# Two transformer blocks on one core: attention values computed transposed, exponentials normalised and gated before their transposes

## The chip, the cores and the metric

The kernel runs on one core of a Trainium2 chip. The metric is the device time of one execution in microseconds (us). Before the change the median of three runs is 2130.94 us (2128.68 to 2131.86).

## The reference, cut to what matters

The program computes two transformer blocks on 512 tokens of width 1024. The first (sliding-window attention, a gated recurrence, retrieval of experts) is not touched. The second projects its normalised input to queries, keys and values of two attentions. In the first one (eight heads of width 64, two groups of keys and values) three softmax branches are added, each with a sigmoid gate per token and head; the compressed branch has 31 keys, and its rows without a valid key give zeros. With 512 tokens and 16 selected blocks of 64 the selected and the window branch are both plain causal attention over all keys.

```python
o_cmp = jnp.einsum('bghsn,bngd->bsghd', p_cmp.astype(vc.dtype), vc)
...
g = jax.nn.sigmoid(gate_logits.astype(jnp.float32)).reshape(B, S, G, HPG, N_BRANCH).astype(q.dtype)
o = g[..., 0:1] * o_cmp + g[..., 1:2] * o_slc + g[..., 2:3] * o_win
...
s = (jnp.einsum('bqhd,bkhd->bhqk', qn, k_nope) + jnp.einsum('bqhd,bkd->bhqk', qr, k_rot)).astype(jnp.float32) * scale
p = masked_softmax(s, key_idx[None, :] <= tc[:, None])
return jnp.einsum('bhqk,bkhd->bqhd', p.astype(v.dtype), v)
...
mixed = jnp.concatenate([o_nsa * jax.nn.silu(z_nsa), o_mla * jax.nn.silu(z_mla)], axis=-1)
x = x + gate[:, None, :] * (mixed @ w_out[l])
return rms_norm_2(x, final_norm_g)
```

The second attention (called MLA) has eight heads with queries and keys of width 96 and values of width 64.

## The kernel before

The second block's attention runs in the trace from about 1793 to 2092 us. Its input `h` lies transposed in two parts, high and low, and every product of `h` with a weight is three matmuls (L105, L106, L107: high·high, low·high, high·low). These are the "fill" records below; they have 512 columns.

Attention is cut into units. A `Unit` is a pair of heads for one tile of 128 queries, `tt`; its keys are the first n = (tt+1)·128. It has three steps. *Scores* (L1371, mask L1373) go into two PSUM banks; VectorE takes the maxima (L1376), ScalarE the exponentials with their sums (L1379, tile `sm_p`). *Turn* transposes the exponentials on TensorE in pieces of 128 keys (L1387) and copies them to SBUF (`sm_pt`; copies alternate between ScalarE, L63, and VectorE, L65). *Values* multiplies the transposed exponentials, as the stationary operand, by the values (L1394), 64 columns for each head and key block, so that the queries come out on the partitions. A `Blocks` unit does the same for the compressed branch with all eight heads at once (L1409, L1413, turn L1429, values L1437 with values laid out block-diagonally by L1689). Sums are inverted after the last unit of a branch (`nsa_done`: reciprocal L1454, gate L1457), and the finished outputs are weighed with them (L1355) and added up by GpSimd (L1463); MLA likewise (L1495, L1497). `mix` transposes the outputs on TensorE (L1548), multiplies them by silu(z) (L1551) and splits them into high and low parts for the output projection.

The order on TensorE is written by hand; the other engines' orders are made by a scheduler from the same program. `attention()` (L1520) takes the units in the order of a table (key tiles 0 and 1, compressed tiles 0 and 1, key 2, compressed 2, MLA 0 and 1, key 3, compressed 3, MLA 2 and 3; a key tile has eight units, an MLA tile four). At each step it issues the turn of the unit before, the scores of the present one, some fill, and the values of the unit two back. The fill is a generator: projections for MLA and the gates, the compressed keys (`blocks`; `fold` L1642 adds position vectors to a projection, L1663 is the hidden layer, its two results on the two column halves), columns of z0, MLA heads (transposes L1709), columns of z1 with a silu at the end (L1803, on ScalarE), the mix of the tiles and the output projection of tiles 0 and 1. `weave_us` draws from it by a number of microseconds that the table gives each unit. The output projection can start only when tiles 0 and 1 of both attentions are mixed. The output projection of tiles 2 and 3 and the last normalisation follow at the end.

Of the kernel before, what the change touches and what calls it, by code (L numbers as in the profile page):

```python
# [17 lines left out]
OP = mybir.AluOpType  # L18
# [1239 lines left out]
def block2(K, x, h, wq, out):  # L1258
    nc, tc, A = K.nc, K.tc, K.A
    with ExitStack() as ctx:  # L1260
# [10 lines left out]
        oN = P.tile([128, NT, 512], F32, name="oN")  # L1271
# [4 lines left out]
        vc = P.tile([128, 2, 4, 64], F32, name="vc")  # L1276
        nc.gpsimd.memset(vc, 0.0)
# [71 lines left out]
        def pair_cols(hh):  # L1349
            j, g = hh % 4, hh // 4  # L1350
            return slice(j * 128 + g * 64, j * 128 + (g + 1) * 64)

        def weigh(dst, o, f):

            nc.vector.tensor_tensor(dst.rearrange("p (j g d) -> p g j d", g=2, d=64),  # L1355
                                    o.rearrange("p (j g d) -> p g j d", g=2, d=64),
                                    f.rearrange("p (g j) -> p g j", g=2)[:, :, :, None].to_broadcast([128, 2, 4, 64]),
                                    op=OP.mult)

        class Unit:  # L1360

            post = needs = None

            def __init__(self, tt, q, k, sums, v, o):
                self.tt, self.q, self.k, self.sums, self.v, self.o = tt, q, k, sums, v, o

            def scores(self):
# [9 lines left out]
                self.p = [T.tile([128, 512], F32, name="sm_p", bufs=2) for _ in range(2)]  # L1377
                for i in range(2):
                    nc.scalar.activation(self.p[i][:, :n], sc[i][:, :n], AF.Exp, bias=m[i], accum_out=self.sums[i])  # L1379
# [11 lines left out]
            def values(self):  # L1391
                for i in range(2):
                    for kb in range(self.tt + 1):
                        nc.tensor.matmul(self.o(i), self.pt[i][:, kb * 128:(kb + 1) * 128], self.v(i, kb), start=kb == 0,  # L1394
                                         stop=kb == self.tt)

        class Blocks:
# [3 lines left out]
            def __init__(self, tt, csum, o):  # L1401
                self.tt, self.csum, self.o = tt, csum, o

            def scores(self):
# [11 lines left out]
                pc = self.pc = T.tile([128, 512], F32, name="sm_p", bufs=2)[:, :256].rearrange("p (j n) -> p j n", n=32)  # L1416
                nc.gpsimd.memset(pc[:, :, NCMP:], 0.0)
                for g in range(2):
                    hs = slice(4 * g, 4 * g + 4)
                    nc.vector.tensor_reduce(cx[:, hs], p3[g], axis=AX.X, op=OP.max)  # L1420
                    nc.vector.tensor_tensor(pc[:, hs, :NCMP], p3[g], cx[:, hs, None].to_broadcast([128, 4, NCMP]),
                                            op=OP.subtract)
                nc.scalar.activation(pc[:, :, :NCMP], pc[:, :, :NCMP], AF.Exp)
                nc.vector.tensor_reduce(self.csum, pc[:, :, :NCMP], axis=AX.X, op=OP.add)

            def turn(self):
                tp = K.bank("tp")
                for g in range(2):
                    nc.tensor.transpose(tp[:, g * 128:(g + 1) * 128],  # L1429
                                        self.pc[:, 4 * g:4 * g + 4].rearrange("p j n -> p (j n)"), K.ident)  # L1430
                self.pt = T.tile([128, 512], F32, name="sm_pt", bufs=2 * LAG + 2)
                K.copy(self.pt[:, :256], tp[:, :256])

            def values(self):
                o = self.o().rearrange("p (j g d) -> p g j d", g=2, d=64)
                for g in range(2):
                    nc.tensor.matmul(o[:, g], self.pt[:, g * 128:(g + 1) * 128], vc[:, g], start=True, stop=True)  # L1437
# [520 lines left out]
```

## Time and profile before

| what | us |
|---|---|
| median of 3 runs | 2130.94 |
| the profiled execution | 2125.71 |
| its span | 2123.9 |
| TensorE busy | 2007.9 |
| VectorE busy | 1558.1 |
| ScalarE busy | 883.4 |

The profiled execution is 5.2 us shorter than the median of the runs, and its span covers all but 1.8 us of it. Engine names in the rows: PE is TensorE's matmul side, PEld its weight loads, DVE VectorE, ACT ScalarE, POOL GpSimd. In a timeline row the number in brackets is the idle time before, with what ended it. Ends of matmuls are modelled, so distances between starts are the better measure.

### The profile page before, as it was taken

To read this page: it belongs to the slowest core of one execution; us is meant where nothing else is said; L and a number is where in the kernel's file an instruction comes from. 1 tells how busy PE (TensorE), PEld (TensorE's weight loads), DVE (VectorE), ACT (ScalarE), POOL (GpSimd) and SP (SyncE) were. 2 spreads that over 40 slices of the span, in tenths; PEclk is the share of its full clock that TensorE was granted. 3 is DMA by queue.
4 is the path that set the end of the run, shared out by engine and by line. 5 is a ranking of instruction groups with operands and counts; after the bars stand their busy time and mean duration, and the time that the engine had idled before them with its cause. 6 is when DMAs were issued, how large, how long until landed. Compare 5 with 4: busy or idle time off the path is not lost.

```text
span 2123.9 us, 29904 instructions
## 1 busy us (share of the span) xinstructions
PE 2007.9 (95%) x11220; PEld 1723.1 (81%) x11220; DVE 1558.1 (73%) x2998; ACT 883.4 (42%) x1368; POOL 489.7 (23%) x408
## 2 busy tenths in 40 slices
PE   8999898999977889999999999999999999989998
PEld 6878676788866878899999999999988877777776
DVE  4457765569999997777777787887878776545557
ACT  4454423333333776333333333333334453444544
POOL 0000001220452000444444444444432101011000
PEclk9999999999988999999999999999999999999999
DMA  4224333442321556998999989999988772211012
GB/s 153 78 79 139 112 117 109 159 139 80 90 80 60 213 214 238 338 328 310 327 329 308 338 304 330 325 315 323 315 292 287 269 236 70 76 40 51 31 51 79
DMA packets 154376, 410.49 MB, mean 193 GB/s; under 512 B 13789, under 2 KB 63733, under 8 KB 150774
## 3 DMA queue, kind: packets, MB, share of 16 engines
q1 hardware_dynamic: 113332, 247.07, 34.4%
q0 software_dynamic: 37440, 136.33, 18.5%
q10 hardware_dynamic: 3458, 25.17, 3.1%
q8 instruction: 88, 1.44, 0.3%
q14 instruction: 58, 0.48, 0.1%
HBM read 378.64 MB, written 29.37 MB: 192 GB/s over the span
## 4 chain that ended last, share of the span: by engine, by line
PE 81%; DVE 12%; ACT 3%; DMA 2%; issue 2%; POOL 1%; ACTq 0%; DVEq 0%; POOLq 0%
PE ps_mm L105 13%; PE ps_mm L106 13%; PE ps_mm L107 13%; PE ps_o L105 7%; PE ps_o L107 6%; PE ps_o L106 6%; PE ps_tp L107 3%; PE ps_tp L106 3%; PE ps_tp L105 3%; PE ps_mm L1000 2%; PE ps_o L1394 2%; PE ps_sc L1371 2%; PE ps_tp L1387 1%; DVE wlo L69 1%; DVE sum L891 1%
## 5 line engine op out<-in xcount | busy, mean ns | idle before, releaser
L68 ACT ACTIVATE whi<-raw 128x1024 fp32r<-128x1024 f32 (+1 forms) x363 | 382.5, 1056 | 658.6 <-issue 429.5
L69 DVE TENSOR_TENSOR wlo<-raw,whi 128x1024 fp32r<-128x1024 f32 (+1 forms) x339 | 415.9, 1229 | 192.5 <-ACT whi L68 191.3
L105 PE MATMUL ps_o<-hT_hi,whi 128*128 128x384 f32 x992 | 342.6, 345 | 13.1 <-ACT act L725 13.1
L107 PE MATMUL ps_o<-hT_hi,wlo 128*128 128x384 f32 x992 | 336.9, 340 | 0.1
L106 PE MATMUL ps_o<-hT_lo,whi 128*128 128x384 f32 x992 | 336.1, 339 | 0.0
L1032 POOL DMA_INDIRECT gath<-in_peer_u_dram,idx x128 | 179.5, 1402 | 376.0 <-DVE junk L1040 181.6
L1032 POOL DMA_INDIRECT gath<-in_peer_v_dram,idx x128 | 176.2, 1376 | 257.0 <-DVE acc L1047 213.6
L105 PE MATMUL ps_mm<-hT_hi,whi 128*128 128x512 f32 (+1 forms) x544 | 222.5, 409 | 0.0
L107 PE MATMUL ps_mm<-hT_hi,wlo 128*128 128x512 f32 (+1 forms) x544 | 216.3, 398 | 0.0
L106 PE MATMUL ps_mm<-hT_lo,whi 128*128 128x512 f32 (+1 forms) x544 | 215.7, 397 | 0.0
L105 PEld LDWEIGHTS ps_o<-hT_hi,whi 128*128 128x128 f32 x992 | 189.8, 191 | 17.2 <-ACT act L725 13.9
L105 PE MATMUL ps_mm<-whi,wh 128*128 128x512 f32 x512 | 200.0, 391 | 2.1 <-ACT wh L68 2.1
L106 PE MATMUL ps_mm<-wlo,wh 128*128 128x512 f32 x512 | 201.6, 394 | 0.4 <-DVE wlo L69 0.4
L107 PE MATMUL ps_mm<-whi,wl 128*128 128x512 f32 x512 | 201.7, 394 | 0.0
L106 PEld LDWEIGHTS ps_o<-hT_lo,whi 128*128 128x128 f32 x992 | 189.6, 191 | 3.3
L107 PEld LDWEIGHTS ps_o<-hT_hi,wlo 128*128 128x128 f32 x992 | 189.1, 191 | 1.0 <-POOL wlo L69 0.6
L1047 DVE SCALAR_TENSOR_TENSOR acc<-gath,w,acc 128x1024 f32<-128x1024 f32 x127 | 162.8, 1282 | 5.6 <-DMA gath<-in_peer_v_dram,idx 3.5
L1040 DVE SCALAR_TENSOR_TENSOR junk<-gath,h 128x1024 bf16<-128x1024 f32 x128 | 156.6, 1223 | 6.8 <-DMA gath<-in_peer_u_dram,idx 4.2
L107 PEld LDWEIGHTS ps_mm<-hT_hi,wlo 128*128 128x128 f32 (+1 forms) x544 | 103.7, 191 | 23.6
L105 PEld LDWEIGHTS ps_mm<-hT_hi,whi 128*128 128x128 f32 (+1 forms) x544 | 103.8, 191 | 21.5 <-ACT dec L508 0.4
L1002 ACT ACTIVATE gst<-ps_mm 128x512 f32<-128x512 f32 x96 | 104.1, 1127 | 40.0 <-PE ps_mm L1000 39.6
L106 PEld LDWEIGHTS ps_mm<-hT_lo,whi 128*128 128x128 f32 (+1 forms) x544 | 103.8, 191 | 20.6 <-DVE hT_lo L69 0.2
(483 smaller groups left out, 3542.5 us busy)
## 6 DMA issues: line engine op xcount, KB each, us to landing
raw<-in_peer_uT_dram SPq DMA_DIRECT2D x128, 512.0 KB
raw<-in_peer_v_dram SPq DMA_DIRECT2D x128, 512.0 KB
raw<-in_w_in_dram SPq DMA_DIRECT2D x59, 512.0 KB
gates_dram<-gst ACTq DMA_DIRECT2D x24, 1024.0 KB
x<-gates_dram SPq DMA_DIRECT2D x32, 768.0 KB
raw<-in_ada_w_dram SPq DMA_DIRECT2D x24, 512.0 KB
raw<-in_w_out_dram SPq DMA_DIRECT2D x24, 512.0 KB
raw<-in_w_peer_q_dram SPq DMA_DIRECT2D x16, 512.0 KB
```

Source lines behind the costliest of these rows:

```text
L68: self.nc.scalar.activation(hi, src, AF.Copy)
L69: (engine or self.nc.vector).tensor_tensor(lo, src, hi.bitcast(F32), op=OP.subtract)
L105: mm(out, a[0], b[0], start=start, stop=False)
L106: mm(out, a[0], b[1], start=False, stop=False)
L107: mm(out, a[1], b[0], start=False, stop=stop)
L1000: nc.tensor.matmul(ps_, hot[:, 1, t // 2, :, t % 2], Ag[:, i, t // 2, :, t % 2], start=i == 0, stop=i == 2)
L1002: nc.scalar.activation(st[:, :, t0:t0 + 4].rearrange("p a t -> p t a"), p.rearrange("p (t a) -> p t a", t=4), AF.Copy)
L1032: nc.gpsimd.indirect_dma_start(out=gath[i], out_offset=None, in_=A["peer_u" if i < NG // 2 else "peer_v"], in_offset=bass.IndirectOffsetOn ...
L1040: nc.vector.scalar_tensor_tensor(junk, g, 1.0, h0, op0=OP.mult, op1=OP.mult, accum_out=act0[:, k:k + 1])
L1047: nc.vector.scalar_tensor_tensor(acc0, g, w0[:, k:k + 1], acc0, op0=OP.mult, op1=OP.add)
L1371: nc.tensor.matmul(sc[i][:, :n], self.q[i], self.k[i], start=True, stop=False)
L1394: nc.tensor.matmul(self.o(i), self.pt[i][:, kb * 128:(kb + 1) * 128], self.v(i, kb), start=kb == 0, stop=kb == self.tt)
```

## The change

Values change operands: the values are the stationary operand (128 keys by 64), the transposed exponentials move (128 columns), and the two heads of a pair write the two halves (`i*64`) of one PSUM bank's partitions, addressed as two column halves of the array. The output thus comes out transposed, with queries on the columns, and all three branches of a tile accumulate in one bank (`Bank`). For that the exponentials must be normalised and gated before they are turned: `Unit.turn` takes the reciprocal of the pair's sums (L1386 in the new file), multiplies by the gate (L1388; not in MLA) and scales each head's exponentials (L1391), then transposes them (L1394). `Blocks.turn` does the same for eight heads and turns them in eight pieces of 31 rows. After the last branch one copy (L65 or L63) takes a tile out of its bank; MLA's bank is read by `mix` itself, which has no transposes any more (L1530). GpSimd's additions, the weighing, the block-diagonal layout (four copies become one) and 12 of 16 matmuls that made it go. In `attention()` the values come before the fill of a step, not after it, and a unit with a gate waits for the gates at its turn, where before only the last unit of a branch waited for them. New lines: scores L1373, mask L1375, maxima L1378, values L1358, `fold` L1621.

```diff
+        class Bank:
+            def __init__(self):
+                self.p = None
+            def add(self, i, cols, v, pt, stop):
+                start = self.p is None
+                if start:
+                    self.p, self.begun = K.bank("o"), set()
+                nc.tensor.matmul(self.p[i * 64:(i + 1) * 64, cols], v, pt, start=i not in self.begun, stop=stop,
+                                 tile_position=(0, i * 64))
+                self.begun.add(i)
...
             def turn(self):
                 n = (self.tt + 1) * 128
+                nc.vector.reciprocal(self.sum, self.sum)
+                if self.gate is not None:
+                    nc.vector.tensor_tensor(self.sum, self.sum, self.gate, op=OP.mult)
                 self.pt = []
-                for p in self.p:
+                for i, p in enumerate(self.p):
+                    nc.vector.tensor_scalar(p[:, :n], p[:, :n], self.sum[:, i:i + 1], None, op0=OP.mult)
                     tp = K.bank("tp")
...
             def values(self):
-                for i in range(2):
-                    for kb in range(self.tt + 1):
-                        nc.tensor.matmul(self.o(i), self.pt[i][:, kb * 128:(kb + 1) * 128], self.v(i, kb), start=kb == 0,
-                                         stop=kb == self.tt)
+                cs = slice(self.pair * 128, (self.pair + 1) * 128)
+                for kb in range(self.tt + 1):
+                    for i in range(2):
+                        self.o.add(i, cs, self.v(i, kb), self.pt[i][:, kb * 128:(kb + 1) * 128], self.last and kb == self.tt)
...
             def turn(self):
-                tp = K.bank("tp")
+                f = T.tile([128, 8], F32, name="cf", bufs=2)
+                nc.vector.tensor_reduce(f, self.pc, axis=AX.X, op=OP.add)
+                nc.vector.reciprocal(f, f)
+                if self.tt == 0:
+                    nc.vector.tensor_scalar(f, f, has, None, op0=OP.mult)
+                nc.vector.tensor_tensor(f, f, branch(self.tt, 0), op=OP.mult)
+                nc.vector.tensor_tensor(self.pc, self.pc, f[:, :, None].to_broadcast([128, 8, NCMP]), op=OP.mult)
...
+        def nsa_done(tt):
+            K.copy(oN[:, tt], banks[tt].p.rearrange("p (j t) -> p j t", j=4))
+            done.add(("nsa", tt))
...
         def attention():
...
-                while u and u.needs and u.needs not in done:
+                while u and u.needs == "blocks" and u.needs not in done:
+                    yield 1.0
+                while line[0] and line[0].needs and line[0].needs not in done:
                     yield 1.0
                 if line[0]:
                     line[0].turn()
                 if u:
                     u.scores()
-                yield u.us if u else 1.0
-                if after:
-                    while "z" not in done:
-                        yield 1.0
-                    after()
-                    after = None
                 if line[LAG]:
                     line[LAG].values()
-                    after = line[LAG].post and line[LAG].post()
+                    yield from line[LAG].post and line[LAG].post() or ()
+                yield u.us if u else 1.0
                 line = [u] + line[:LAG]
...
         def mix(tt, o, k0):
-            p = K.bank("tp")
-            for j in range(4):
-                nc.tensor.transpose(p[:, j * 128:(j + 1) * 128], o[:, j * 128:(j + 1) * 128], K.ident)
...
-            nc.vector.tensor_tensor(mt, p.rearrange("p (j t) -> p j t", j=4), late["z"][k0 // 4][:, :, ts], op=OP.mult)
+            nc.vector.tensor_tensor(mt, o, late["z"][k0 // 4][:, :, ts], op=OP.mult)
```

The order on VectorE in key tile 3, from one unit's copy to the next unit's, before (`sm_pt` is the turned tile, `nm` the maxima, `sums` the branch's sums, `wlo` a weight's low part):

```order
L65 COPY sm_pt<-ps_tp 128x512 [waits DVE_49,PE_49]
L1376 TENSOR_REDUCE nm<-ps_sc 128x1 [waits PE_49] x2
L65 COPY sm_pt<-ps_tp 128x512 [waits DVE_49,PE_49]
L1376 TENSOR_REDUCE nm<-ps_sc 128x1 [waits PE_49] x2
L1454 RECIPROCAL sums<-sums 128x8 [waits Activation_49]
L1457 TENSOR_TENSOR sums<-sums,gates 128x8 [waits DVE_49]
L69 TENSOR_TENSOR wlo<-raw,whi 128x1024 [waits DMAHW7_49,Activation_49]
L65 COPY sm_pt<-ps_tp 128x512 [waits PE_49]
```

and after (`sm_s` holds the pair's sums):

```order
L65 COPY sm_pt<-ps_tp 128x512 [waits PE_49]
L1378 TENSOR_REDUCE nm<-ps_sc 128x1 [waits PE_49] x2
L1386 RECIPROCAL sm_s<-sm_s 128x2 [waits Activation_49]
L1388 TENSOR_TENSOR sm_s<-sm_s,gates 128x2 [waits DVE_49]
L1391 TENSOR_SCALAR sm_p<-sm_p,sm_s 128x512 [waits DVE_49]
L1391 TENSOR_SCALAR sm_p<-sm_p,sm_s 128x512
L69 TENSOR_TENSOR wlo<-raw,whi 128x1024 [waits DMAHW6_49,Activation_49]
L65 COPY sm_pt<-ps_tp 128x512 [waits PE_49]
```

Reciprocal, gate and two scales now stand in every unit between the maxima and the next copy; before, reciprocal and gate stood there once in four units.

TensorE's order where the z1 columns end (the `ps_mm` records are the last of z1), before:

```order
L107 MATMUL ps_mm<-hT_hi,wlo 128x512
L1548 MATMUL ps_tp<-ident,oN 128x128 x8
L1548 MATMUL ps_tp<-ident,otmp 128x128 x4
L1394 MATMUL ps_o<-vm,sm_pt 128x64 x4
L1387 MATMUL ps_tp<-ident,sm_p 128x128 x4
L1371 MATMUL ps_sc<-kF,qF 128x256 x2
L1373 LDWEIGHTS identb
L1373 MATMUL ps_sc<-cmask,identb 128x128
L1373 LDWEIGHTS identb
L1373 MATMUL ps_sc<-cmask,identb 128x128
L1394 MATMUL ps_o<-vm,sm_pt 128x64 x4
```

and after:

```order
L105 MATMUL ps_mm<-hT_hi,whi 128x512
L106 MATMUL ps_mm<-hT_lo,whi 128x512
L107 MATMUL ps_mm<-hT_hi,wlo 128x512
L1394 MATMUL ps_tp<-ident,sm_p 128x128 x2
L1373 MATMUL ps_sc<-kF,qF 128x128 x2
L1375 LDWEIGHTS identb
L1375 MATMUL ps_sc<-cmask,identb 128x128
L1375 LDWEIGHTS identb
L1375 MATMUL ps_sc<-cmask,identb 128x128
L1358 MATMUL ps_o<-sm_pt,vm 64x128 x2
L1394 MATMUL ps_tp<-ident,sm_p 128x128 x2
L1373 MATMUL ps_sc<-kF,qF 128x256 x2
```

Before, the transposes of the mix stand behind the last z1 record, and the units that follow are the last two of MLA tile 1 (256 keys); after, the mix has no records, and the units that follow are the last of MLA tile 0 (128 columns) and then all four of tile 1. Up to the next fill record come five turns before and seven after.

The order on VectorE around `fold` of the first projection, before (`ab`, `abx` are its results):

```order
L65 COPY sm_pt<-ps_tp 128x128 [waits PE_49]
L1376 TENSOR_REDUCE nm<-ps_sc 128x1 [waits PE_49] x2
L1642 TENSOR_TENSOR ab<-ps_mm,cp 64x248 [waits PE_49]
L1642 TENSOR_TENSOR abx<-ps_mm,cp 64x248 [waits DMAHW6_49]
L1642 TENSOR_TENSOR ab<-ps_mm,cp 64x248
L1642 TENSOR_TENSOR abx<-ps_mm,cp 64x248
L1642 TENSOR_TENSOR abx<-ps_mm,cp 64x248 [waits DMAHW7_49]
L1642 TENSOR_TENSOR ab<-ps_mm,cp 64x248
L1642 TENSOR_TENSOR abx<-ps_mm,cp 64x248
L1642 TENSOR_TENSOR ab<-ps_mm,cp 64x248
L1454 RECIPROCAL sums<-sums 128x8 [waits Activation_49]
```

and after:

```order
L1388 TENSOR_TENSOR sm_s<-sm_s,gates 128x2 [waits DVE_49]
L1391 TENSOR_SCALAR sm_p<-sm_p,sm_s 128x128 [waits DVE_49]
L1621 TENSOR_TENSOR ab<-ps_mm,cp 64x248 [waits PE_49]
L1621 TENSOR_TENSOR abx<-ps_mm,cp 64x248 [waits DMAHW6_49]
L1621 TENSOR_TENSOR ab<-ps_mm,cp 64x248
L1621 TENSOR_TENSOR abx<-ps_mm,cp 64x248
L1621 TENSOR_TENSOR abx<-ps_mm,cp 64x248 [waits DMAHW7_49]
L1621 TENSOR_TENSOR ab<-ps_mm,cp 64x248
L1621 TENSOR_TENSOR abx<-ps_mm,cp 64x248
L1621 TENSOR_TENSOR ab<-ps_mm,cp 64x248
L65 COPY sm_pt<-ps_tp 128x128 [waits PE_49]
L1391 TENSOR_SCALAR sm_p<-sm_p,sm_s 128x128
```

The eight additions, which wait for a projection on TensorE, stood between a unit's maxima and the reciprocal of a branch, and no transposes waited behind them; now they stand between the scales of a unit's first and second head.

## Rows read from the trace of the kernel before

**Rows 1.** the page: head, and TensorE's busy time, share and instructions.

```profile
span 2123.9 us, 29904 instructions
...
PE 2007.9 (95%) x11220; PEld 1723.1 (81%) x11220; DVE 1558.1 (73%) x2998; ACT 883.4 (42%) x1368; POOL 489.7 (23%) x408
```

**Rows 2.** windows (us, busy us and instructions of each engine, TensorE's granted clock, DMA).

```profile
1975.00:2010.00 35.00, 30.01 (x179) 22.61 (x178) 18.98 (x35) 19.89 (x45) 0.00 (x0) 0.90 0.10 31
2010.00:2094.00 84.00, 83.58 (x546) 66.66 (x546) 50.57 (x88) 42.41 (x94) 2.65 (x3) 1.00 0.16 51
```

**Rows 3.** timeline, one key-3 unit (start us, us, engine, line, operation, count).

```profile
2016.66 1.04 PE L1387 MATMUL ps_tp<-ident,sm_p 128*128 128x128 f32 x8
...
2018.96 1.29 DVE L1376 TENSOR_REDUCE nm<-ps_sc 128x1 f32<-128x512 f32 x2 [0.53 <-PE ps_sc L1373]
...
2020.27 1.89 PE L1394 MATMUL ps_o<-vn,sm_pt 128*128 128x64 f32 x16
...
2020.99 0.20 ACT L1379 ACTIVATION_READ_ACCUMULATOR sm_p<-ps_sc,nm 128x1 f32 x1
...
2022.00 0.39 PE L1387 MATMUL ps_tp<-ident,sm_p 128*128 128x128 f32 x2
```

**Rows 4.** pieces of the chain that ended last (start us, us, engine, tile, line).

```profile
1845.66 0.23 PE ps_mm L107
1845.89 0.39 PE ps_o L1394 x4
...
1848.82 2.11 PE ps_mm L1663 x32
...
1922.60 0.86 PE ps_o L1437 x4
...
2078.97 0.44 PE ps_tp L1548 x4
2079.41 1.73 PE ps_o L1394 x16
```

**Rows 5.** VectorE's groups by form (xcount | busy us, mean ns | idle before).

```profile
L1642 DVE TENSOR_TENSOR ab<-ps_mm,cp 64x248 f32<-64x248 f32 x8 | 3.3, 410 | 3.4 <-PE ps_mm L107 3.4
...
L1454 DVE RECIPROCAL sums<-sums 128x8 f32<-128x8 f32 x12 | 2.4, 202 | 8.0 <-ACT sm_p L1379 7.9
...
L1457 DVE TENSOR_TENSOR sums<-sums,gates 128x8 f32<-128x8 f32 x12 | 2.0, 168 | 0.3
...
L326 DVE TENSOR_SCALAR lf<-lf,omlb,lb 128x512 f32<-128x512 f32 x4 | 2.0, 544 | 1.0 <-ACT lf L324 1.0
...
L328 DVE TENSOR_SCALAR kh<-lf 128x512 f32<-128x512 f32 x4 | 1.5, 420 | 0.0
```

**Rows 6.** timeline, a unit of 256 keys.

```profile
1976.27 0.39 PE L1387 MATMUL ps_tp<-ident,sm_p 128*128 128x128 f32 x2
...
1977.62 0.76 DVE L1376 TENSOR_REDUCE nm<-ps_sc 128x1 f32<-128x256 f32 x2
...
1978.96 0.20 ACT L1379 ACTIVATION_READ_ACCUMULATOR sm_p<-ps_sc,nm 128x1 f32 x1
```

**Rows 7.** timeline after the last z1 column.

```profile
1987.33 1.28 ACT L1803 ACT_TABLE_LOAD   x1
...
1988.62 1.91 ACT L1803 ACTIVATE z<-z 128x2048 f32<-128x2048 f32 x1
...
1991.89 0.44 PE L1387 MATMUL ps_tp<-ident,sm_p 128*128 128x128 f32 x2 [2.51 <-ACT sm_pt L63]
...
1994.18 1.28 ACT L1379 ACT_TABLE_LOAD   x1 [0.54 <-DVE nm L1376]
```

**Rows 8.** window after that stop.

```profile
1992.00:2000.00 8.00, 7.36 (x31) 4.76 (x32) 3.79 (x9) 3.32 (x7) 0.00 (x0) 0.57 0.02 6
```

**Rows 9.** TensorE's weight loads of L1663 (xcount | busy us, mean ns | idle).

```profile
L1663 PEld LDWEIGHTS ps_mm<-w,ab 128*62 128x62 f32 x64 | 4.0, 207 | 0.5 <-PE ps_mm L106 0.4
```

**Rows 10.** the chain where TensorE ends.

```profile
2115.28 0.25 PE ps_mm L107
```

More of the change, by code (lines that the diff above doesn't have):

```diff
@@ L1347, in block2, with __init__ @@
                       + full([W[17 + c] for c in range(4)]) + wo + wo, 3)
[L1349 to L1358, printed above, removed]
+        class Bank:
[8 more added lines that the diff above has]
+                self.begun.add(i)
         class Unit:
-            post = needs = None
-            def __init__(self, tt, q, k, sums, v, o):
-                self.tt, self.q, self.k, self.sums, self.v, self.o = tt, q, k, sums, v, o
+            post = needs = gate = None
+            def __init__(self, tt, q, k, v, o, pair, last):
+                self.tt, self.q, self.k, self.v, self.o, self.pair, self.last = tt, q, k, v, o, pair, last
             def scores(self):
@@ L1451, in nsa_done @@
-        def nsa_done(tt, br, o):
-            gl = gates[:, tt].rearrange("p (h b) -> p b h", b=3)
-            f = sums[:, tt, br]
-            nc.vector.reciprocal(f, f)
-            if br == 0 and tt == 0:
-                nc.vector.tensor_scalar(f, f, has, None, op0=OP.mult)
-            nc.vector.tensor_tensor(f, f, gl[:, br], op=OP.mult)
-            if br == 1:
-                weigh(oN[:, tt], o(), f)
-            else:
-                tmp = T.tile([128, 512], F32, name="otmp", bufs=2)
-                weigh(tmp, o(), f)
-                nc.gpsimd.tensor_tensor(oN[:, tt], oN[:, tt], tmp, op=OP.add)
-            if br == 0:
-                done.add(("nsa", tt))
+                    self.o.add(g, slice(0, 512), vc[:NCMP, g * 64:(g + 1) * 64], self.pt[g][:NCMP], True)
@@ L1467, in key_units, with branch @@
+        def branch(tt, br):
+            return gates[:, tt].rearrange("p (h b) -> p b h", b=3)[:, br]
+        banks = [Bank() for _ in range(NT)]
+        def nsa_done(tt):
+            K.copy(oN[:, tt], banks[tt].p.rearrange("p (j t) -> p j t", j=4))
+            done.add(("nsa", tt))
         def key_units(tt):
@@ L1470, in key_units @@
             for br in range(2):
-                o = shared_bank()
                 for j in range(4):
@@ L1489, in mla_units @@
             ts = slice(tt * 128, (tt + 1) * 128)
[L1490 to L1491 removed]
+            o = Bank()
             kF, qF, vm = late["heads"]
             def finish():
[L1495 to L1499 removed]
+                while "z" not in done:
+                    yield 1.0
+                mix(tt, o.p.rearrange("p (j t) -> p j t", j=4), 4)
+                done.add(("mla", tt))
             for h0 in range(0, MLA_H, 2):
```

74 lines of the change are left out of this document (24 added, 50 removed).

## The prediction

> **What bounds the kernel now.** I read the page first: the profiled execution's span is 2123.9 us and TensorE is busy for 2007.9 us of it, 95% [rows 1]. So TensorE's own work sets the time nearly everywhere, and an idle engine elsewhere costs nothing. The share is an average, though, and the change touches only the second block's attention, so next I read windows of that part [rows 2]: from 1975 to 2010 us TensorE is busy only 30.01 of 35 us (granted clock 0.90), from 2010 to 2094 it is full, 83.58 of 84. The reader is to see that the last stretch is bound by TensorE in one execution, but not with how much to spare. For that I took one unit (a pair of heads of a 512-key tile) from the timeline [rows 3]: TensorE starts its transposes at 2016.66 and the next unit's at 2022.00, a period of 5.34. Inside it runs a chain through three engines: scores, maxima on VectorE from 2018.96 (2.30 after the turn began), exponentials on ScalarE, the second one's sum read out at 2021.19 (2020.99 + 0.20), that is 2.23 after the maxima began. Then 0.81 us pass until the next turn, in which the values L1394 still run on TensorE. This 0.81 is all the slack that the chain has.
>
> **The change part by part.** Median of the runs 2130.94, this execution 2125.71; the sum is made against the execution, and 5.2 is added at the end.
>
> *Values.* Before, 16 records take 1.73 and 4 take 0.39 to 0.43, about 0.108 each [rows 4]. After, as many records go in twos on column halves, with 128 moving columns. The trace has that form once, L1663: 32 records in 2.11 [rows 4]. Set as 16 pairs, with 0.18 for entering and leaving, it is 0.121 a pair: units of one to four key blocks cost 0.42, 0.66, 0.90 and 1.14 instead of 0.43, 0.86 (twice 0.43), 1.30 and 1.73. With 12 units of each size the gain is 12 × (0.01 + 0.20 + 0.38 + 0.59) = 14.2 us of TensorE work. The other end: no overlap of halves, 0.108 a record as now, gain nothing.
>
> *Other TensorE work.* The 32 transposes of the mix, 0.44 for four [rows 4], go: −3.5. Each of four block units turns eight small pieces instead of two (+6 × 0.11 = 0.66, ×4 = +2.6), and its values go from 0.86 [rows 4] to two records on halves with 512 columns, which I take at 1.06 (bounds 0.46, two L105 fill records, and 1.72, twice the row): +0.8. In all −14.3 us on TensorE.
>
> *What stands before the transposes now.* A turn used to need only the exponentials. Now VectorE first takes the reciprocal (0.20, as L1454), multiplies by the gate (0.17, as L1457; not in MLA) and scales each head's 512 exponentials. That multiply is not in the trace with this operand; L328 (0.42) and L326 (0.54, two scalars per partition) are the bounds, I take 0.48 [rows 5]. The first head must be scaled before the transposes begin, the second runs beside them. With 0.1 for two hand-overs the chain from the maxima to the next turn grows from 2.23 to 2.23 + 0.20 + 0.17 + 0.48 + 0.10 = 3.18; in MLA 2.98. For 256 keys the row is 1.54 (1977.62 to 1979.16, [rows 6]), plus 0.17 to 0.20, a scale of 0.3 and the hand-overs: 2.17 without gate.
>
> That exceeds the slack. A 512-key unit after has TensorE work of 2.30 up to the maxima, and beside the chain only values 1.14 and six fill records 1.40 (0.23 each [rows 4]), 2.54 against 3.18. So the chain sets the period, 2.30 + 3.18 = 5.48 against 5.34: the 0.59 saved in such a unit buys an idle TensorE and 0.14 is lost on top. The saving counts where there is more fill, in the early tiles.
>
> *First stretch, key tiles 0 and 1.* Fill is plentiful and the chain hidden. Values: key 0 8 × +0.03 (0.42 against the lower 0.39) = +0.3, key 1 8 × −0.18 = −1.4, the smaller compressed-value products −0.2. But in VectorE's new order the eight L1642 (L1621 after; 0.41 each [rows 5]) stand between the two scales of one unit, and they wait for a projection whose last six TensorE records come just before this unit's turn. The second head's transposes wait for eight of them, some 8 × 0.37 = 3.0 us, of which 0.8 lies under the first half of the turn: +2.2. Bounds 0 and 3.3. Sum +0.9.
>
> *Second stretch, blocks 0 and 1, key 2, block 2.* Values 8 × −0.38 = −3.0; block units +0.6 (values) and +2.0 (turns, three of them); VectorE's copies of the MLA keys come to stand between reciprocal and scale, +1.0 (bounds 0 and 3). Sum +0.6.
>
> *Third stretch, from the last z1 record to TensorE's end.* Attention starts its second unit later (it waits for the gates), so at the end of the z1 columns it is four units further back than before, some 6.2 us of work that before had done by then. After these columns the fill has nothing to give until the first MLA tiles are mixed, and the order shows six steps in a row without fill (seven turns) where there were four (five turns). Their period is the chain's. First, ScalarE needs a table load (1.28), the silu (1.91) and a load back (1.28) [rows 7] ahead of the next exponentials; with 1.2 before them (the silu's load began 1.2 after the fill's end at 1986.1) and 0.8 for two short exponentials with their sums the next turn comes about 6.45 after the last z1 record, of which TensorE stands idle for 5. Then four units of 256 keys at 1.6 (1976.27 to 1977.62, and two transposes more, [rows 6]) + 2.17 = 3.8, one step with four transposes and 512-key scores 5.0, one of 5.5: 32.2 us until the turn of the second key-3 unit. To that I add 2.3 for the clock: the trace shows 0.57 granted in 1992 to 2000 [rows 8], that is mostly 1.2 GHz, after a stop of 2.51 [rows 7], and it cost 7.36 × 0.43 = 3.2 us there; after, less of the stretch is TensorE's. From that turn to the end: six key units × 5.48 = 32.9, block 5.2, MLA tile 2 20.7 (384 keys, 4.9 to 5.8 a unit by the same rule), MLA tile 3 26.3 (two units by the chain, 5.7 and 5.9, and two of 7.3 that carry 15 output records more each), and what follows 19.0 (66 output records at 0.235, where before 96 stood, and 3.5 for the last values): 104. Sum 138.5. Before: from 1986.1 to 2115.5 [rows 10] 129.4, and the 6.2 of the four units: 135.6. Difference +2.9, with the mix transposes and the smaller values already inside.
>
> *Sum.* 0.9 + 0.6 + 2.9 = +4.4: 2125.7 + 4.4 = 2130.1 for a profiled execution, 2135.3 for the median. From −14.3 of work some 18.7 are paid back, nearly all as waits for VectorE and ScalarE.
>
> **A rule beside the row.** The 32 weight loads of L1663 take 0.207 each by their own row [rows 9], 6.6 us in sum, and yet the group lasts 2.11: the loads hide under the products. The Trainium skill, "TensorE: Matmul & The Clock Gate", Part 3 (What overlaps and what doesn't), says that a weight load runs beside a product in flight only when their row groups differ; two column halves share all rows. By that rule the pairs would gain nothing, which is the third rival below; the row, 0.121 for a pair of products and two loads, speaks against it here.
>
> **Rivals.**
>
> *One: the chain fits.* If the scale takes 0.42 or less and the hand-overs nothing, and if the fill (which the scheduler may spread otherwise than I read it) covers what is left, the second and third stretch are TensorE-bound again. Then −14.3 of work shows but for the z1 stop (+5) and half the fold (+1): −8, 2123. For it: before runs full from 2010 to 2094. Against it: slack 0.81, addition 0.95.
>
> *Two: the clock stays low (slower).* Before, a stop of 2.51 us was followed by 0.57 of the clock over 8 us [rows 7, 8]. After, the stop is 5 us and the six steps after it leave TensorE idle about half of the time. If the clock stays at 1.2 GHz until the fill returns, the TensorE part of each step (1.6 to 2.3 us) doubles: six × 1.9 = 11 instead of 2.3, so 2135.3 + 8.7 = 2144. It decides from the point where the clock is not back by the second of these steps. Against it: from 2010 on the clock was full [rows 2], after a stretch that had no fill either (it returned at about 2012).
>
> *Three: the halves do not run together.* Values stay at 0.108 a record: the early stretches lose 4.4, the last one little (the chain covers it) beyond MLA tile 3, 1: 2141.
>
> *Four: gains and losses cancel.* The fold and the MLA copies find cover (0.5 instead of 3.2) and z1's stop is 1.5 shorter: 2131.
>
> **How the numbers follow.** The measurement tells 0.2% (4.3 us) from no change. Chances: the forecast 0.43 (its own range 2131 to 2140), one 0.23, two 0.14, three 0.07, four 0.13. Faster (under 2126.7): rival one and a little of four, 0.24. Same: rest of four and a good third of the forecast, 0.28. Slower: 0.48. The range 2121 to 2147 reaches over rivals one to three.
>
> **What the profile after would show.** Right: the scale L1391 128x512 between 0.42 and 0.54; unit periods of 5.4 to 5.6 in key 3 with TensorE idle ahead of the transposes, released by VectorE's sm_p; 16 value records in about 1.14; a stop of about 5 us after the z1 silu; TensorE busy under 80 of 84 us in the last stretch. Wrong: key 3 units at 5.0 or less (rival one), a clock near 0.5 over 20 us (two), 16 value records in 1.7 (three). I would be wrong above all if the six steps without fill take less than 3 us each, or if the scale is much cheaper than any row here.

## The result

The changed kernel takes 2151.3 us (median of 4 runs, 2147.4 to 2153.1) against 2129.8 for the kernel before (median of 4, three of them those shown above); the ratio is 1.0099, 95% interval 1.0078 to 1.0120. The profiled execution takes 2147.36 us, 21.7 more than the one before. The direction was as forecast, the size was not: forecast was +4.4 us, and the time lies above the range.

The head of the profile after, to be read against [rows 1]:

```profile
span 2145.6 us, 30004 instructions
...
PE 2004.8 (93%) x11200; PEld 1695.3 (79%) x11200; DVE 1590.1 (74%) x3145; ACT 888.7 (41%) x1372; POOL 475.6 (22%) x395
```

TensorE is busy 3.1 us less, in a span that is 21.7 longer. Windows of the same stretches as [rows 2]:

```profile
1975.00:2010.00 35.00, 24.29 (x142) 17.65 (x142) 18.80 (x54) 17.60 (x45) 0.00 (x0) 0.85 0.09 30
2010.00:2094.00 84.00, 72.03 (x491) 47.15 (x490) 54.13 (x114) 36.32 (x83) 0.00 (x0) 0.98 0.14 45
```

The stretch that was full (83.58 of 84) now has 12 us of stops. The list of what TensorE waited for (total us, times, longest) begins, from 1788 us on, before:

```profile
PE ps_mm L105 <- ACT qm L1717: 3.5, 1, 3.5
PE ps_tp L1387 <- ACT sm_p L1379: 3.4, 4, 1.4
PE ps_tp L1387 <- ACT sm_pt L63: 2.5, 1, 2.5
```

and after (L1391 is the scale, L1394 the transposes, L1221 the rotation of MLA's key part):

```profile
PE ps_tp L1394 <- DVE sm_p L1391: 26.2, 19, 5.9
PE ps_mm L105 <- ACT qm L1692: 3.2, 1, 3.2
PE ps_tp L1394 <- DVE kr L1221: 2.8, 1, 2.8
```

Nineteen turns wait for the scale, 26.2 us in all; before, four turns waited 3.4 for exponentials.

**Where the time went, as a sum.** I cut the attention stage, from the last transposes of the queries (about 1799) to TensorE's last product, into windows of 1 us. In each, idle is its length less TensorE's busy time, and the price of the clock is the busy time × (1 − granted clock); the rest is work at full clock. (One execution each; us.)

| kernel | stage | idle | clock | rest |
|---|---|---|---|---|
| before | 317.0 | 15.6 | 6.5 | 294.8 |
| changed | 337.0 | 39.1 | 13.3 | 284.6 |
| no scale | 314.0 | 18.9 | 13.6 | 281.4 |
| turn one step later | 312.5 | 20.1 | 9.5 | 282.9 |
| before, with scale | 353.2 | 35.9 | 20.4 | 296.9 |
| old order in a step | 353.5 | 43.7 | 28.0 | 281.8 |
| scale twice | 373.9 | 58.6 | 32.2 | 283.1 |
| later turn, head by head | 323.3 | 19.0 | 13.5 | 290.7 |
| changed, with fill products | 341.2 | 35.1 | 16.1 | 290.0 |

So the change saves 10.2 us of work and pays 23.5 in stops and 6.8 in clock: +20.0 in the stage, and the last normalisation ends 1.1 later behind TensorE.

**One step, read as in [rows 3].** Timeline after, a key-3 unit (rows between left out):

```profile
2050.72 1.09 PE L1358 MATMUL ps_o<-sm_pt,vn 128*64 128x128 f32 x16
2050.77 1.29 DVE L1378 TENSOR_REDUCE nm<-ps_sc 128x1 f32<-128x512 f32 x2
...
2051.74 0.50 PE L105 MATMUL ps_mm<-whi,hT_hi 128*128 128x512 f32 x1
...
2052.80 0.20 ACT L1382 ACTIVATION_READ_ACCUMULATOR sm_p<-ps_sc,nm 128x1 f32 x1
...
2053.03 0.17 DVE L1386 RECIPROCAL sm_s<-sm_s 128x2 f32<-128x2 f32 x1 [0.98 <-ACT sm_p L1382]
2053.23 0.16 DVE L1388 TENSOR_TENSOR sm_s<-sm_s,gates 128x2 f32<-128x2 f32 x1
2053.44 0.69 DVE L1749 TENSOR_TENSOR mt<-ps_mm,grow 128x512 f32<-128x512 f32 x1
2054.05 0.87 DVE L1391 TENSOR_SCALAR sm_p<-sm_p,sm_s 128x512 f32<-128x512 f32 x2
...
2054.67 1.06 PE L1394 MATMUL ps_tp<-ident,sm_p 128*128 128x128 f32 x8 [1.27 <-DVE sm_p L1391]
```

From the maxima to the sum it is 2.23 (2050.77 to 2053.00), as before. Reciprocal, gate and scale follow, and here a residual of the output projection (L1749, 0.69) as well, which VectorE's order has put between gate and scale. The next turn comes 3.90 after the maxima, where [rows 3] have 3.04. The 16 value records take 1.02 (2050.72 to 2051.74), even less than the 1.14 forecast, and the time is spent waiting. Of the six steps that follow the second unit's turn, three take 5.62, the two with a residual 6.23, and one 6.32, in which the low part of a weight (L69, 1.23) stands ahead of a copy and the maxima (before: 5.34).

### The profile page after: what moved, and what is told of

Read it like the earlier page. It is cut to its first block, busy times and chain, and to the rows that moved or that the text cites. A ratio compares the mean times of both kernels' runs of the same rounds, so it can differ in the third digit from the quotient of the medians.

```text
span 2145.6 us, 30004 instructions
## 1 busy us (share of the span) xinstructions
PE 2004.8 (93%) x11200; PEld 1695.3 (79%) x11200; DVE 1590.1 (74%) x3145; ACT 888.7 (41%) x1372; POOL 475.6 (22%) x395
## 4 chain that ended last, share of the span: by engine, by line
PE 78%; DVE 14%; ACT 4%; DMA 2%; issue 2%; POOL 1%; ACTq 0%; DVEq 0%; POOLq 0%
PE ps_mm L105 13%; PE ps_mm L106 13%; PE ps_mm L107 13%; PE ps_o L105 7%; PE ps_o L107 6%; PE ps_o L106 6%; PE ps_tp L107 3%; PE ps_tp L105 3%; PE ps_tp L106 3%; PE ps_mm L1000 3%; PE ps_sc L1373 2%; DMA raw<-in_ada_w_dram 2%; DVE wlo L69 1%; PE ps_tp L1394 1%; PE ps_o L1358 1%
## 5 line engine op out<-in xcount | busy, mean ns | idle before, releaser
L69 DVE TENSOR_TENSOR wlo<-raw,whi 128x1024 fp32r<-128x1024 f32 (+1 forms) x339 | 415.1, 1226 | 181.3 <-ACT whi L68 178.2
```

The source lines that it names most:

```text
L69: (engine or self.nc.vector).tensor_tensor(lo, src, hi.bitcast(F32), op=OP.subtract)
```

## The experiments

The diffs are against the changed kernel, one against the kernel before, as its heading says. All times are medians; the ratio is to the kernel before, timed beside it on the same chip. Beside the experiments the kernel before has medians of 2130.2 to 2133.4 (2129.8 beside the changed kernel), so two kernels are better compared by their ratios, and where the intervals of these overlap the difference is not certain.

**The scale left out.**

```diff
-                nc.vector.reciprocal(self.sum, self.sum)
-                if self.gate is not None:
-                    nc.vector.tensor_tensor(self.sum, self.sum, self.gate, op=OP.mult)
...
-                    nc.vector.tensor_scalar(p[:, :n], p[:, :n], self.sum[:, i:i + 1], None, op0=OP.mult)
```

> The changed kernel without reciprocal, gate and scale ahead of a unit's transposes (key tiles and MLA; that part of the result is left out), all else as changed: values transposed, column halves, the loop's order, the wait for the gates. Theory W (the loss is TensorE waiting for VectorE's scale): the trace of the changed kernel has 26 us of stops released by the scale, and some 3 us of half clock behind them; both go, 2151 becomes about 2123 (2118 to 2129). Rival C (column halves as a form, or the clock, cost the time whatever is scaled): stays above 2140.

Measured 2122.7, ratio 0.9953 [0.9937, 0.9968]. The waits of its trace (L1390 are its transposes):

```profile
PE ps_tp L1390 <- ACT sm_p L1382: 8.2, 6, 4.9
```

Without these four small VectorE instructions in a unit (three in MLA) the same kernel is 28.5 us faster (31 by the ratios). Rival C falls: values transposed on column halves cost no time by themselves. What is left are waits for exponentials, 4.9 of them behind the z1 silu. By the table the gain is stops (20.2 us less idle) and not clock: half clock costs this kernel as much (13.6) as the changed one (13.3), against the expectation that some of it would go too.

**The turn one step later.** The scale stays, and the unit's chain gets a whole step more. The wait for the gates moves along with the turn, and the pairs' sums get four buffers too.

```diff
-                if line[0]:
-                    line[0].turn()
+                if line[1]:
+                    line[1].turn()
                 if u:
                     u.scores()
-                if line[LAG]:
-                    line[LAG].values()
+                if line[LAG + 1]:
+                    line[LAG + 1].values()
...
-                self.p = [T.tile([128, 512], F32, name="sm_p", bufs=2) for _ in range(2)]
+                self.p = [T.tile([128, 512], F32, name="sm_p", bufs=4) for _ in range(2)]
```

> The changed kernel with every turn (and the values) one step later, so that a unit's chain of maxima, exponentials and scale has a whole step more; four buffers of exponentials instead of two. Theory W: the chain is hidden, most of the 26 us of stops go, the stop behind the z1 silu shortens by about a step; about 2126 (2120 to 2132). Rival T (VectorE is at its throughput in the steps without fill): stops stay, 2138 or more.

Measured 2124.5, ratio 0.9967 [0.9951, 0.9983]: faster than both kernels, as theory W expected. What TensorE still waits for the scale:

```profile
PE ps_tp L1394 <- DVE sm_p L1391: 0.3, 1, 0.3
```

Its timeline in key 3:

```profile
2021.98 1.04 PE L1394 MATMUL ps_tp<-ident,sm_p 128*128 128x128 f32 x8
2022.09 0.88 DVE L1391 TENSOR_SCALAR sm_p<-sm_p,sm_s 128x512 f32<-128x512 f32 x2
...
2024.22 1.09 PE L1358 MATMUL ps_o<-sm_pt,vn 128*64 128x128 f32 x16
...
2026.73 0.49 PE L1394 MATMUL ps_tp<-ident,sm_p 128*128 128x128 f32 x3
```

A unit takes 4.75, which is 5.34 less 0.59, the forecast saving of a unit's values. The scale at 2022.09 is that of the next unit and nobody waits for it. No run tries the four buffers without the later turn; in the changed kernel, though, ScalarE's exponentials wait for nothing but the maxima (L1378, 51.4 us in all), so no buffer was missing there.

**The scale in the kernel before.**

```diff
+                nc.vector.reciprocal(sm, self.both)
+                if self.needs2:
+                    nc.vector.tensor_tensor(sm, sm, sm, op=OP.mult)
                 for i, p in enumerate(self.p):
+                    nc.vector.tensor_scalar(p[:, :n], p[:, :n], sm[:, i:i + 1], None, op0=OP.mult)
```

> The kernel before, with its old values, and in every unit a reciprocal, a small product and the two scales ahead of the transposes (the result is normalised twice). Theory W: the chain grows by 0.9 us; units of key 3 go from 5.34 to about 5.5, the four steps without fill grow by 0.9 each and the fold stands in the way once: before + 8 (5 to 12). Rival C: before, within 4 us.

Measured 2166.6, ratio 1.0173 [1.0145, 1.0201], +33 by the medians where 8 were expected. The direction is as in theory W, the size far off, so my chain was too short here too. In one of its steps, from the timeline (L1399 are its values, L1392 its transposes):

```profile
2045.15 1.89 PE L1399 MATMUL ps_o<-vn,sm_pt 128*128 128x64 f32 x16
...
2046.26 0.16 DVE L1387 TENSOR_TENSOR sm_s<-sm_s 128x2 f32<-128x2 f32 x1
2047.09 0.69 DVE L1355 TENSOR_TENSOR oN<-ps_o,sums 128x512 f32<-128x512 f32 x1 [0.66 <-PE ps_o L1399]
2047.69 0.87 DVE L1389 TENSOR_SCALAR sm_p<-sm_p,sm_s 128x512 f32<-128x512 f32 x2
2048.32 1.06 PE L1392 MATMUL ps_tp<-ident,sm_p 128*128 128x128 f32 x8 [1.27 <-DVE sm_p L1389]
```

VectorE's next instruction in order is the weighing of a finished branch; it waits for TensorE's values, the scale waits behind it, and TensorE's turn waits for the scale. The step that ends with this turn costs 1.2 more than the two that follow (6.79 against 5.56).

**The old order in a step** (fill first, then values).

```diff
+                yield u.us if u else 1.0
                 if line[LAG]:
                     line[LAG].values()
                     yield from line[LAG].post and line[LAG].post() or ()
-                yield u.us if u else 1.0
```

> The changed kernel with the old order in a step: fill first, values behind it. Theory W: nothing but places on TensorE moves, the chain is as long: within 4 us of the changed kernel's 2151. Rival L (the new place of the values costs, since the fill comes later): 2145 or less.

Measured 2160.8, ratio 1.0134 [1.0108, 1.0160], 9.5 slower than the changed kernel by the medians and 7.5 by the ratios, whose intervals overlap a little. Rival L falls: the new place of the values is not what costs. Theory W's 4 us are exceeded, though by these intervals not with certainty. The table says where the time went: idle is 4.6 more, clock 14.7 more. A window of its trace:

```profile
1996.00:2024.00 28.00, 19.44 (x80) 12.59 (x80) 12.47 (x34) 10.25 (x32) 0.00 (x0) 0.51 0.01 4
```

After the stop behind the z1 silu the clock stays at 1.2 GHz through all steps without fill. This is the prediction's second rival, in this kernel and not in the changed one (0.58 in its worst 12 us).

**No wait for the gates at the start.**

```diff
-                    u.gate, u.needs = branch(tt, 1 + br)[:, j::4], "gates"
+                    u.gate, u.needs = (branch(tt, 1 + br)[:, j::4], "gates") if tt else (None, None)
```

> The changed kernel with no gate in the units of key tile 0 (left out there, their reciprocal and scale stay), so that attention need not wait for the gates before its second unit. Theory W with the late start as a part of it: the stop of 2.8 us at the first turn and the half clock behind it (about 1.7) go, and the order then has three steps without fill ahead of key 3 instead of six, some 1.6 us of stop and clock each: 2151 becomes about 2141 (2136 to 2145). Rival S (the late start only shifts work, the scale is all): 2148 to 2152.

Measured 2145.5, ratio 1.0072 [1.0044, 1.0101]: 5.8 better than the changed kernel by the medians, between theory W and rival S. The intervals of the ratios overlap, so that the late start is a part of the loss is likely and not shown; it is at most a small one. The waits for the scale still sum to 24.7, since the z1 stop, now 7.1 long, has only moved to a larger unit.

**Both scales ahead of the transposes.**

```diff
                 for i, p in enumerate(self.p):
                     nc.vector.tensor_scalar(p[:, :n], p[:, :n], self.sum[:, i:i + 1], None, op0=OP.mult)
+                for p in self.p:
                     tp = K.bank("tp")
```

> The changed kernel with both scales of a unit written ahead of both heads' transposes, so that VectorE takes nothing between them. Theory W: the 2.1 us stop at the fold goes, the first head waits no longer than before: 2148 (2145 to 2151). Rival F (the second scale delays copies and maxima): 2153 or more.

Measured 2150.1, ratio 1.0093 [1.0064, 1.0122], no difference that can be told from 2151.3. The run decides nothing, since the edit did not do what it says: the scheduler still put the eight additions (L1622 here) between the two scales. From its timeline:

```profile
1846.71 0.29 DVE L1391 TENSOR_SCALAR sm_p<-sm_p,sm_s 128x128 f32<-128x128 f32 x1
...
1846.94 0.41 DVE L1622 TENSOR_TENSOR ab<-ps_mm,cp 64x248 f32<-64x248 f32 x1
...
1849.35 0.42 DVE L1622 TENSOR_TENSOR ab<-ps_mm,cp 64x248 f32<-64x248 f32 x1
1849.78 0.29 DVE L1391 TENSOR_SCALAR sm_p<-sm_p,sm_s 128x128 f32<-128x128 f32 x1
...
1850.21 0.30 PE L1395 MATMUL ps_tp<-ident,sm_p 128*128 128x128 f32 x1 [1.80 <-DVE sm_p L1391]
```

**The scale twice.**

```diff
                     nc.vector.tensor_scalar(p[:, :n], p[:, :n], self.sum[:, i:i + 1], None, op0=OP.mult)
+                    nc.vector.tensor_scalar(p[:, :n], p[:, :n], 1.0, None, op0=OP.mult)
```

> The changed kernel with each scale followed by a second one, by 1.0 (the suspected cost doubled). Theory W: each of some 25 turns that wait for the scale waits 0.3 to 0.45 longer, +8 to +14 with some clock: about 2162. Rival C: within 4 us of 2151.

Measured 2181.2, ratio 1.0236 [1.0207, 1.0265]: +30, twice and more what theory W expected. The waits for the scale:

```profile
PE ps_tp L1395 <- DVE sm_p L1392: 45.9, 27, 7.4
```

19.7 us more of stops, and 18.9 more of half clock by the table. Stops and clock grow together here: in the steps without fill 0.53 was granted from 2000 to 2022 us of this execution, and at that clock TensorE's part of a step, on which the chain hangs, is longer too. Leaving out reciprocal, gate and scales gave 28.5, and adding a second scale per head alone cost 30, although it is the shorter piece of chain (0.3 to 0.5 us for the first head). So the price of a microsecond of chain is not fixed here: the longer chain makes more turns wait (27 for 19) and pays 18.9 in clock, while leaving the scale out saved no clock.

**Values head by head, with the later turn.**

```diff
-                for kb in range(self.tt + 1):
-                    for i in range(2):
+                for i in range(2):
+                    for kb in range(self.tt + 1):
```

> The changed kernel with the turn one step later, and in a unit's values first all key blocks of one head, then all of the other, so that neighbouring records lie on the same column half. It shows what the halves side by side are worth once the chain is hidden. Theory H (records on one half run one after the other, about 0.108 each or more): the values lose what they had gained, some 14 us of TensorE work, of 2124.5 becomes 2137 (2132 to 2142). Rival P (the pace is the same, or the gain is off the path anyway): within 4 us of 2124.5.

Measured 2134.1, ratio 1.0006 [0.9989, 1.0023], 9.6 slower than with the halves in turn (8.3 by the ratios, whose intervals are apart): theory H, with a smaller size than 14. TensorE's values in the two traces, first head by head:

```profile
L1358 PE MATMUL ps_o<-sm_pt,vn 128*64 128x128 f32 x320 | 31.1, 286 | 0.0
```

and with the halves in turn:

```profile
L1358 PE MATMUL ps_o<-sm_pt,vn 128*64 128x128 f32 x320 | 24.5, 283 | 0.0
```

In key 3 a unit takes 5.24 instead of 4.75, its 16 records 1.51 instead of 1.02. By the table 7.8 of the 11.9 us of work that the later turn saves are gone with it, and against the kernel before no gain is left. The gain of the change is thus mostly the two halves at work together, and it shows in the time only where the chain is hidden.

**Spread fill, and products that nobody reads.** Three kernels that try to win back the rest. The first takes the turn one step later, the gates as ready one projection later, and less early fill (of its diff, the fill):

```diff
-FB = (2.2, 1.6, 1.1, 0.8, 0.7, 0.7)
+FB = (1.9, 1.3, 1.0, 0.8, 0.7, 0.7)
```

> The changed kernel with every turn one step later (as in the earlier run), the gates taken as ready only after the next projection, and less fill given to the early units (1.9, 1.3, 1.0 in the table instead of 2.2, 1.6, 1.1), so that three steps without fill are left instead of six. Theory W: of the later turn's 2124.5 the stop for the gates (3.7) and about half of the stops and half clock around the z1 silu (8) go: about 2117 (2112 to 2122). Rival N (what stands there only moves): 2123 to 2127.

Measured 2121.3 (2118.1 to 2129.5), ratio 0.9961 [0.9946, 0.9976]: the median lies at the upper end of theory W's range, but it is not told apart from the plain later turn (0.9967), so neither theory is settled. The others put a product into each step without fill:

```diff
                 while tt == 1 and ("mla", 1) not in done:
-                    yield None
+                    nc.tensor.matmul(K.bank(), K.ident, late["heads"][2][:, 0], start=True, stop=True)
+                    yield 1.6
```

> The changed kernel with one product of 512 columns that nobody reads (0.86 us) behind the values in each of the six steps without fill. It adds 5.2 us of TensorE work into stops that wait for VectorE. Theory K (the clock is a loss of its own there, behind the stops): the granted clock in the stretch from 1994 to 2018 is back to full two or three steps earlier, 2151 becomes 2147 (2144 to 2151). Rival A (work added is time added): 2155 or more.

> The kernel with the turn one step later, with the same product in its four steps without fill. Theory K: half clock around the z1 silu cost it some 5 us, of which 2 to 3 come back, and the added 3.4 us lie in stops of 3.5: 2124.5 becomes 2123 (2120 to 2126). Rival A: 2127 or more.

> The kernel with the later turn, gates taken later and less early fill, with the same product in its steps without fill. In its profiled run half clock cost 17 us, more than in any other kernel with the later turn. Theory K: 2121 becomes 2118 (2114 to 2121) and the runs lie closer together. Rival A: 2123 or more.

Measured 2151.0 (changed kernel, ratio 1.0090 [1.0062, 1.0117]), 2122.6 (later turn, 0.9961 [0.9945, 0.9977]) and 2122.1 (spread, 0.9958 [0.9940, 0.9975]). None moved its kernel by more than can be told: the added work was not added time (rival A falls for the first two, the third lies between the theories), and theory K's gain does not show either. In the changed kernel the clock did come back earlier; the windows, without the products:

```profile
1994.00:2006.00 12.00, 7.12 (x29) 4.87 (x30) 6.40 (x19) 5.34 (x18) 0.00 (x0) 0.58 0.00 2
2006.00:2024.00 18.00, 12.49 (x83) 7.67 (x82) 9.84 (x24) 6.59 (x21) 0.00 (x0) 0.91 0.01 1
```

and with them:

```profile
1994.00:2006.00 12.00, 8.13 (x31) 4.62 (x32) 6.12 (x19) 6.60 (x19) 0.00 (x0) 0.72 0.09 33
2006.00:2024.00 18.00, 13.03 (x82) 7.01 (x82) 10.44 (x28) 7.17 (x21) 0.00 (x0) 1.00 0.01 1
```

So the added work (5.4 us by the table) lay for the most part in stops (4.0 less idle), as theory K says, but the clock won there is only 1.8 us (7.12 × 0.42 + 12.49 × 0.09 less 8.13 × 0.28), and by the table half clock elsewhere took more than that back in this execution (16.1 for 13.3).

## Why the prediction was wrong

For the stretch behind the z1 columns the mechanism was right: the chain through VectorE sets the period, and the saved work buys idle time. The sizes failed, nearly all in one direction, and in the first stretches a stop and a fall of the clock were missing altogether. The profiled execution takes 17.3 us more than the 2130.1 forecast for it: 7.1 stand ahead of the last z1 record, 9.1 between it and TensorE's end, 1.1 in the last normalisation.

*TensorE's work.* Forecast −14.3, measured −10.2 in the changed kernel and −11.9 with the later turn (the rest column). That column is good to some 3 us: kernels with the same TensorE instructions (changed, no scale, old order, scale twice) read 281.4 to 284.6. The values themselves gained more than forecast: by the distances of starts at full clock, units of one to four key blocks take 0.37, 0.59, 0.81 and 1.02 for 0.39, 0.84, 1.28 and 1.73 before, 12 × (0.02 + 0.25 + 0.47 + 0.71) = 17.4 us for 14.2. Where TensorE lost some of it again is not taken apart. That the later turn's units are shorter by just the forecast 0.59 is therefore partly luck: their values save 0.71. Three sums of the prediction are off by 0.02 to 0.03 us (0.38 for 1.30 − 0.90, 2.98 for 3.01, 2.17 for 2.14), which is too little to matter.

*The scale.* Forecast 0.48 for 512 exponentials, and the forms after say 481 ns, with the two small ones close to their rows of before:

```profile
L1391 DVE TENSOR_SCALAR sm_p<-sm_p,sm_s 128x512 f32<-128x512 f32 x24 | 10.6, 481 | 0.3
...
L1386 DVE RECIPROCAL sm_s<-sm_s 128x2 f32<-128x2 f32 x48 | 7.9, 164 | 35.3 <-ACT sm_p L1382 35.1
...
L1388 DVE TENSOR_TENSOR sm_s<-sm_s,gates 128x2 f32<-128x2 f32 x32 | 5.1, 161 | 1.0
```

*The first two stretches, forecast +1.5: the step that failed first.* The last z1 record was to come at about 1981.4 (1986.1 − 6.2 + 1.5); it ends at 1988.5. I counted the late start through the gates only as a shift of the fill. It is a stop as well, which no term had (the row names VectorE's last small instruction before the turn, L1221; the turn reads the scaled exponentials of L1391, which wait for the gates):

```profile
1810.65 0.25 ACT L1571 ACTIVATE gates<-ps_tp 128x96 f32<-128x96 f32 x1
...
1811.14 0.15 DVE L1388 TENSOR_TENSOR sm_s<-sm_s,gates 128x2 f32<-128x2 f32 x1
...
1811.48 0.27 DVE L1391 TENSOR_SCALAR sm_p<-sm_p,sm_s 128x128 f32<-128x128 f32 x1
...
1811.90 0.58 PE L1394 MATMUL ps_tp<-ident,sm_p 128*128 128x128 f32 x2 [2.78 <-DVE kr L1221]
```

The attention resumes as soon as the gates are issued, not when they are there: the turn stands in TensorE's order before the fill that could have covered them. The clock falls behind it, and again in key 0. The same windows, first before:

```profile
1812.00:1816.00 4.00, 4.00 (x25) 3.26 (x24) 3.09 (x16) 1.88 (x5) 1.45 (x6) 1.00 0.49 135
1836.00:1840.00 4.00, 4.00 (x22) 3.35 (x21) 1.39 (x7) 2.12 (x6) 0.00 (x0) 1.00 0.32 98
1840.00:1844.00 4.00, 4.00 (x23) 3.13 (x23) 3.01 (x10) 2.08 (x6) 0.00 (x0) 1.00 0.01 2
```

and after:

```profile
1812.00:1816.00 4.00, 4.00 (x16) 2.95 (x17) 3.02 (x20) 2.37 (x6) 1.81 (x8) 0.63 0.21 83
1836.00:1840.00 4.00, 4.00 (x19) 3.61 (x19) 2.01 (x8) 0.00 (x0) 0.00 (x0) 0.61 0.29 64
1840.00:1844.00 4.00, 4.00 (x18) 2.47 (x17) 1.69 (x4) 1.43 (x2) 0.00 (x0) 0.53 0.02 4
```

These three windows cost 4.9 us (4 × 0.37 + 4 × 0.39 + 4 × 0.47), where the kernel before had full clock; with the 2.8 of the stop, and the 0.5 by which this execution was late already at 1798, they more than account for the 7.1 that were missing. The two windows in key 0 (3.4 of the 4.9) are partly bad luck: other executions kept the clock there, as the last section shows. The stop at the fold was right in size (2.2 forecast, 2.1) and in its place between the two scales.

*The third stretch, forecast 138.5 us, measured 147.6.* From the last z1 record at 1988.5 to the second key-3 unit's turn it took 36.8 where I had 32.2 + 2.3 (the turn after the silu alone came at 7.2, not 6.45: table loads and silu were right, but I left out reciprocal and scale behind them):

```profile
1988.52 0.38 PE L1394 MATMUL ps_tp<-ident,sm_p 128*128 128x128 f32 x2
...
1995.72 0.66 PE L1394 MATMUL ps_tp<-ident,sm_p 128*128 128x128 f32 x2 [5.89 <-DVE sm_p L1391]
```

From there to TensorE's end it took 110.8 for 104. Units with nothing but the chain were forecast well (5.62 for 5.48, 256 keys 3.90 for 3.8). What was missing, and stood at nothing in the sum, is everything else that VectorE does in that order: the residual between gate and scale (+0.61 in two units) and the weight's low part in key 3, whose six steps took 35.6 for 32.9; in MLA tile 3 (28.4 for 26.3) the mix, residuals and a weight's low part stand ahead of a unit's maxima or scale. The remaining 2.0 I did not take apart. Half clock behind the silu cost 4.8 (1993 to 2018 us, as in the table) where the sum has 2.3. I had read the order for such places only where a queue of eight stood there.

*The rivals.* One (the chain fits) is what happens when the scale is taken out or the turn comes a step later (2122.7, 2124.5; its 2123 was for that state). Two (clock) is a part: 6.8 of 30.3 us paid, but mostly not where I looked: 1.7 behind the wait for the gates, 3.4 in key 0 and only 1.7 behind the z1 silu; and the kernel without scale pays as much. Three is refuted by 1.02 us for 16 records. In it I had gone from loads that cannot hide to pairs that gain nothing, and left out that two products may run side by side, which they do. What stays open: why half clock is granted in one execution and not in a neighbour with nearly the same stops; and where the idle time of the kernels with the later turn (20 us, 4.5 more than before) could still be turned into time, since neither spreading fill nor filling stops moved the medians measurably.

## What to carry to other kernels

Work moved off a full engine is worth its time only where the chain that feeds that engine has slack for what is put into it; take one step's chain and slack first, and then give the chain a step more (a second pair of buffers, one step of delay) before counting the saving. An instruction put between two engines' hand-overs costs what stands around it in its engine's queue, not only its own duration: read that queue's order in every kind of step. And read the granted clock behind stops that grow: the doubled scale paid 18.9 us in it, while taking the scale out gave none back.

## What the runs showed of the hardware that I had not expected

Products on two column halves run side by side. With the later turn the single records of a key-3 unit's values start in pairs, 6 ns apart within a pair and 0.109 us from pair to pair, so that 16 records of 128 columns pass in 1.02 us, with a new weight load for each. Head by head, a half that works alone has the same 0.109 from record to record; the 16 take 1.51, and not the 1.74 of sixteen in a row, since by the starts the second head's records begin 0.49 after the first head's, before those are through. The values of a block show it too: four records of 512 columns, two on each half, pass in 1.00, where before four of 256 columns in a row took 0.86 [rows 4]. By that row a record of 128 columns takes about 0.108 alone (an estimate, 0.86 / 8), so the second product of a pair and both its loads fit into the time of one product, although both halves use all rows. The Trainium skill, "TensorE: Matmul & The Clock Gate", Part 3 (What overlaps and what doesn't), has a weight load beside a product in flight only where the row groups differ; these runs differ from it, and the measurement decides.

TensorE's clock fell to 1.2 GHz with no stop ahead of it. In the changed kernel's timeline it falls about 2 us after the one-column products of the norms begin; the two slow windows (0.61 and 0.53) shown above are the ones from there:

```profile
1834.79 3.19 PE L1587 MATMUL ps_tp<-ones,sq 128*128 128x1 f32 x24
```

TensorE counts as busy all the way. Of the fourteen profiled executions ten lost the clock within 2 to 5 us of the start of these 24 products, among them those without scale and with the old order (without the wait for the gates, half a microsecond of idle time lies between); four kept it: the kernel before, the scale in the kernel before, both scales first, and the later turn. The later turn with fill products, whose edit differs from the plain one's only in products that come later, lost it. So the order of instructions alone does not decide it, and what does stays open.
